# A hybrid decoder block: one column of blocks goes from the seven-product scheme to plain products, and the state space steps get another order and a third buffer

## The chip, the cores and the metric

The kernel runs on one core of one Trainium2 chip, in float32. The metric is the time on the device in microseconds (us). The engines are PE (TensorE, matmuls), DVE (VectorE), ACT (ScalarE), POOL (GpSimd) and SP (SyncE, which here only issues DMAs). Each works through its own queue in the order in which the program is written; they wait for each other by semaphores.

## The reference

One decoder block over 1024 positions of width 1024. The part that matters here is the mixer:

```python
def mixer_block(xn, ...):
    proj = jnp.einsum('bsd,de->bse', xn, w_in) + b_in
    u_ssm, c_bgate, c_cgate, c_val, g_ssm, g_conv = jnp.split(proj, SPLIT_POINTS, axis=-1)
    y_ssm = s5_branch(u_ssm, ...)                       # diagonal state space scan, 32 groups of 64 states
    z = jax.nn.gelu(y_ssm)
    y_a = (z @ w_glu_a) * jax.nn.sigmoid(z @ w_glu_b)
    y_b = (c_bgate * causal_short_conv(c_cgate * c_val, conv_w, conv_b)) @ w_conv_out
    merged = jax.nn.sigmoid(g_ssm) * y_a + jax.nn.sigmoid(g_conv) * y_b
    return merged @ w_out
```

Before it stands an RMS norm, after it a residual, a second norm, a squared-ReLU MLP of width 4096 and a last norm.

## The kernel before

**Exact products from split operands.** Every float32 operand is cut into a high part (an ACT copy with rounding) and a low part (a DVE subtraction). A product of two blocks is three matmuls of 128x512: high by high, high by low, low by high (lines 135 to 137 in `products`, 885 to 887 in `chain`).

**Plain jobs.** `order` lists jobs (`u` 3, then `gs`, `gc`, `bg`). A job multiplies one 128-column block of `w_in` (tile `wr`, cut into `wh` on ACT at line 95 and `wl` on DVE at line 96) with all of x: 48 matmuls into two banks `ps`. Jobs 0 and 1 use the operands `xg` from the start of the kernel. Between them `normed_in` loads x once more, multiplies it by the norm (line 1068) and cuts it into the tiles `xhwB`/`xlwB` (lines 744 and 736) which jobs 2 to 22 use.

**Work beside the products.** The generators `cut_u` and `ssm_step` are drawn piece by piece between matmuls. Each `yield` with a positive number is a declared cost in us, paid out of a credit that grows with the matmuls at the rate `BESIDE` of the job; a negative number is a distance in PE time that must pass first. What is left when the last job begins is written out in one piece by `drain`.

**State space.** `ssm_params` is a chain of some 200 small POOL operations (16 or 32 columns) on columns of one tile, `scratch`, which comes from the same pool of 34 tiles (`unit`, 128x1024) as the operands; so do the small tiles `iota_i` and `bbt`. A tile taken from a pool waits until the last reader of its former owner is done. `cut_u` then copies the first four jobs' results into `U` with 32 copies on ACT and 32 on DVE. Each of eight `ssm_step`s writes its small matrices `Bk` and `Vk` on POOL (`outer`, lines 463 to 467), its angles on DVE and ACT, transposes on PE (`pst`, with `psk` beside it), copies them on ACT (`WT`, `Mk`), projects on PE (`psxr`, `psxi`), rotates and scans on DVE (lines 527 to 540), rotates back (lines 543 to 545 on POOL, 546 to 548 on DVE) and forms its output on PE (`psy`). Step s+1 is started when the projection of step s has been written.

**Groups of seven products.** The other weight blocks go four at a time through a scheme with seven block products (`P1` to `P7`) in place of eight: a group is 84 matmuls. There are two groups (`val`, `cg`) for each of four columns m, a gate group, and four groups for the convolution's output matrix (`rg<-in_wco`). Their operands are sums of blocks; those of the convolution (`xcd`) are made by `conv_first` and `conv_second`, one step after each product, cut into two parts, sent through DRAM by POOL's queue and read back by `xc_load` on SP's queue at the places that `XC_LOADS` names. `group_load` loads a group's raw weights, two groups ahead.

Of the kernel before, what the change touches and what calls it, by code (L numbers as in the profile page):

```python
# [30 lines left out]
PREPARE = 38.0  # L31
N_WARM = 9

BESIDE = {"u": 0.4, "gs": 0.8, "gc": 0.8, "bg": 0.8}
# [12 lines left out]
def block_kernel(ctx, tc, x_t, par, ssm, w_u, win, wco, wglu, wo, w1, w2, out):  # L47
# [97 lines left out]
    order = [("u", 3)] + [("gs", i) for i in range(7)] + [("gc", i) for i in range(7)] + [("bg", i) for i in range(8)]  # L145
    base = {"u": 0, "bg": 4, "cg": 12, "val": 20, "gs": 28, "gc": 36}
# [73 lines left out]
    def cut_u():  # L220
        for b in range(4):
            u = unit(f"U{b}").rearrange("p (q c) -> p q c", q=4)
            tv = ut[b].rearrange("p (c j) -> p j c", j=CH)
            for q in range(4):
                for j in range(CH):
                    o, i = u[32 * j:32 * j + 32, q, :], tv[32 * q:32 * q + 32, j, :]
                    bias = pt[32 * q:32 * q + 32, C_BIN + b:C_BIN + b + 1]
                    if (q + j) % 2:
                        A.activation(o, i, AF.Identity, bias=bias)
                    else:  # L230
                        V.tensor_scalar(o, i, bias, None, op0=ALU.add)
                yield 0.6
            U[b] = u
# [5 lines left out]
    def sp(name, w=NQ):  # L239
        if name not in names:  # L240
            if name in ("th", "tl", "mags"):
                names[name] = spool.tile([P, w], F32, name=f"sp_{name}")
            else:
                o = scratch["used"]
                scratch["used"] = o + w
                names[name] = scratch["t"][:, o:o + w]
        return names[name]
# [10 lines left out]
    Vk2 = [spool.tile([P, 2, 2, 160], F32, name=f"Vk{i}") for i in range(2)]  # L258
    Mk2 = [spool.tile([P, 2, P], F32, name=f"Mk{i}") for i in range(2)]
# [48 lines left out]
    def ssm_params():  # L308
        scratch["t"] = unit("scratch")
        nc.sync.dma_start(bc_raw, ssm.rearrange("p (f q c) -> p f q c", f=4, q=NQ))  # L310
        ii = unit("iota_i").bitcast(I32)[:, :NC]
# [103 lines left out]
        u1 = unit("bbt")[:, :NQ * 16].rearrange("p (q c) -> p q c", q=NQ)  # L415
# [32 lines left out]
    def ssm_step(s):  # L448

        q = slice(2 * s, 2 * s + 2)  # L450
        Vk, Mk = Vk2[s % 2], Mk2[s % 2]
# [21 lines left out]
        yield -3.0  # L473
# [40 lines left out]
        for m in range(4):  # L514
            A.activation(Mk[32 * m:32 * m + 32, :, 32 * m:], pk[:, :, :P - 32 * m], AF.Copy)
        yield -4.0
# [6 lines left out]
        if s < 7:  # L523
            start(ssm_step(s + 1))
# [17 lines left out]
        yr, t2, t3 = sh(f"yr{s}"), sh(f"t2{s}"), sh(f"t3{s}")  # L542
        G.tensor_tensor(t2, xr, sn, op=ALU.mult)  # L543
        G.tensor_tensor(t3, xi, cs, op=ALU.mult)
        G.tensor_tensor(t3, t3, t2, op=ALU.add)
# [4 lines left out]
        yield -6.0  # L550

        py = bank(f"psy{s}")
        for i in range(2):
            o = i * NC
            T.matmul(py[:, o:o + NC], Mk[:, i, :], u_of(2 * s + i), start=True, stop=False)
            for r, y in ((0, yr), (1, t3)):
# [135 lines left out]
    xcd = {(nm, part): scratch_of(f"xc{nm}{part}", (P, 4, HALF)) for nm in X_OF.values() for part in "hl"}  # L692
# [265 lines left out]
    def to_xc(m, name, t, lo=None):  # L958
        split_out(f"xc{name}{m}", lambda part: xcd[name, part][:, m, :], t, lo)
# [31 lines left out]
    def done_cg(m, quad, ps, less):  # L991
# [10 lines left out]
        elif quad == "c21":  # L1002
            conv.append(conv_second(m))
# [37 lines left out]
    for m in range(4):  # L1041
# [49 lines left out]
    for n in range(n_main):  # L1091
# [30 lines left out]
        if n >= n_main - 4:  # L1122
            sums_load(n - (n_main - 4))
        if k == "u":
# [24 lines left out]
    def xc_load(name, u):  # L1149
        ts = []  # L1150
        for part in "hl":
# [4 lines left out]
        xc[name, u] = ts  # L1156

# [20 lines left out]
    for n in range(first_f1):  # L1178
        preps = [group_steps(n, 1), group_steps(n + 1, 0) if n + 1 < first_f1 else iter(())]

        def after(i):
            for prep in preps:
                next(prep, None)
            for _ in range(2 if n == first_co - 1 and i in (1, 2) else 1):
                conv_step()
            step_on()
            for name, u in XC_LOADS.get(7 * (n - first_co + 1) + i, []):
                xc_load(name, u)
            if n >= first_co and i == 1:
                gate_load(n - first_co)  # L1190
            if i == 6 and n + 2 < first_f1:
                group_load(n + 2)
# [522 lines left out]
```

## Time and profile before

| | us |
|---|---|
| median of three runs (lowest, highest) | 1559.28 (1557.91, 1562.05) |
| the profiled execution's own time | 1562.93 |
| its span in the profile | 1560.8 |

The span is the stretch from the first to the last instruction; 2.1 us of the execution lie around it. The profile's page gives busy time by engine, then forty slices of 39 us each; further views give single stretches, waits, and instructions in order of time. The mean of a PE instruction in these views is longer than the distance between two of them, since matmuls are pipelined; the distance between starts is what a matmul costs.

### The profile page before, as it was taken

To read this page: it belongs to the slowest core of one execution; us is meant where nothing else is said; L and a number is where in the kernel's file an instruction comes from. 1 tells how busy PE (TensorE), PEld (TensorE's weight loads), DVE (VectorE), ACT (ScalarE), POOL (GpSimd) and SP (SyncE) were. 2 spreads that over 40 slices of the span, in tenths; PEclk is the share of its full clock that TensorE was granted. 3 is DMA by queue.
4 is the path that set the end of the run, shared out by engine and by line. 5 is a ranking of instruction groups with operands and counts; after the bars stand their busy time and mean duration, and the time that the engine had idled before them with its cause. 6 is when DMAs were issued, how large, how long until landed. Compare 5 with 4: busy or idle time off the path is not lost.

```text
span 1560.8 us, 17513 instructions
## 1 busy us (share of the span) xinstructions
PE 1439.8 (92%) x6407; PEld 1183.6 (76%) x6407; DVE 1026.0 (66%) x1459; ACT 621.7 (40%) x903; POOL 305.1 (20%) x562
## 2 busy tenths in 40 slices
PE   9757999999489997599999999999999999999997
PEld 7645778787368886487888888888888778787887
DVE  7551757777778887155663588777776355858576
ACT  6245345333454444122331245444333342424254
POOL 5860351635102111000000001222222101000000
PEclk9968999999689999799999999999999999999999
DMA  5612212223043556955542124555556658736212
GB/s 205 209 61 90 72 67 96 68 84 146 27 148 140 184 181 251 363 201 197 207 174 104 58 85 137 176 179 186 178 182 233 241 188 200 257 97 254 94 50 100
DMA packets 80518, 240.84 MB, mean 154 GB/s; under 512 B 10160, under 2 KB 18736, under 8 KB 80432
## 3 DMA queue, kind: packets, MB, share of 16 engines
q1 hardware_dynamic: 52016, 158.97, 29.7%
q0 software_dynamic: 18624, 61.88, 11.2%
q10 hardware_dynamic: 9792, 18.88, 3.1%
q8 instruction: 50, 0.82, 0.2%
q14 instruction: 36, 0.29, 0.1%
HBM read 158.94 MB, written 80.74 MB: 154 GB/s over the span
## 4 chain that ended last, share of the span: by engine, by line
PE 71%; DVE 8%; POOL 8%; DMA 5%; ACT 4%; issue 3%; SPq 0%; ACTq 0%; DVEq 0%; POOLq 0%
PE seed L885 6%; PE seed L887 6%; PE seed L886 6%; PE pa L887 4%; PE pa L885 4%; PE pa L886 4%; PE pe L885 4%; PE pe L887 4%; PE pe L886 4%; PE ps L135 2%; PE ps L137 2%; PE ps L136 2%; PE pw L135 2%; PE pw L137 2%; PE pw L136 2%
## 5 line engine op out<-in xcount | busy, mean ns | idle before, releaser
L136 PE MATMUL ps<-xlwB,wh 128*128 128x512 f32 x336 | 136.9, 407 | 20.1 <-DVE xlwB L736 20.1
L135 PE MATMUL ps<-xhwB,wh 128*128 128x512 f32 x336 | 140.3, 418 | 15.8 <-ACT wh L95 11.2
L137 PE MATMUL ps<-xhwB,wl 128*128 128x512 f32 x336 | 135.9, 405 | 0.6 <-DVE wl L96 0.5
L857 DVE TENSOR_TENSOR gl<-gs,gh 128x1024 fp32r<-128x1024 f32 x78 | 95.0, 1218 | 11.0 <-ACT gh L853 11.0
L853 ACT ACTIVATE gh<-gs 128x1024 fp32r<-128x1024 f32 x78 | 82.3, 1055 | 34.4 <-DVE gs L849 27.1
L136 PEld LDWEIGHTS ps<-xlwB,wh 128*128 128x128 f32 x336 | 66.2, 197 | 35.9 <-DVE xlwB L736 22.4
L135 PEld LDWEIGHTS ps<-xhwB,wh 128*128 128x128 f32 x336 | 66.3, 197 | 33.1 <-ACT wh L95 12.0
L96 DVE TENSOR_TENSOR wl<-wr,wh 128x1024 fp32r<-128x1024 f32 x23 | 29.6, 1286 | 78.4 <-ACT wh L95 78.4
L137 PEld LDWEIGHTS ps<-xhwB,wl 128*128 128x128 f32 x336 | 66.3, 197 | 16.0 <-DVE wl L96 1.7
L857 DVE TENSOR_TENSOR gl<-rg,gh 128x1024 fp32r<-128x1024 f32 (+1 forms) x78 | 72.1, 950 | 5.3 <-ACT gh L853 4.6
L896 ACT ACTIVATE seed<-pa 128x512 f32<-128x512 f32 x39 | 22.7, 582 | 117.5 <-PE pa L887 117.1
L853 ACT ACTIVATE gh<-rg 128x1024 fp32r<-128x1024 f32 (+1 forms) x78 | 62.8, 838 | 0.4 <-ACT e L1135 0.4
L1135 ACT ACTIVATE e<-ps,pt 128x512 f32<-128x512 f32 x42 | 28.8, 687 | 59.1 <-PE ps L137 54.2
L543 POOL TENSOR_TENSOR t<-xr,sn 128x512 f32<-128x512 f32 x8 | 12.0, 1506 | 200.6 <-DVE xr L540 200.6
L135 PE MATMUL pw<-mh,hwo 128*128 128x512 f32 x128 | 49.9, 390 | 0.0
L137 PE MATMUL pw<-mh,lwo 128*128 128x512 f32 x128 | 49.8, 389 | 0.0
L136 PE MATMUL pw<-ml,hwo 128*128 128x512 f32 x128 | 49.8, 389 | 0.0
L885 PE MATMUL seed<-xhft,gh 128*128 128x512 f32 x112 | 44.4, 397 | 3.3 <-DVE holdc L1487 3.3
L886 PE MATMUL seed<-xlft,gh 128*128 128x512 f32 x112 | 44.2, 395 | 0.0
L887 PE MATMUL seed<-xhft,gl 128*128 128x512 f32 x112 | 44.1, 394 | 0.0
L887 PE MATMUL pa<-xhfB,gl 128*128 128x512 f32 x112 | 43.6, 389 | 0.0
L886 PE MATMUL pa<-xlfB,gh 128*128 128x512 f32 x112 | 43.6, 389 | 0.0
(648 smaller groups left out, 4311.1 us busy)
## 6 DMA issues: line engine op xcount, KB each, us to landing
rg<-in_w SPq DMA_DIRECT2D x52, 512.0 KB, 4.5
wr<-in_win SPq DMA_DIRECT2D x23, 512.0 KB, 3.5
rg<-in_win SPq DMA_DIRECT2D x18, 512.0 KB, 4.2
xn<-in_x_t SPq DMA_DIRECT2D x16, 256.0 KB, 4.3
xnd<-xn ACTq DMA_DIRECT2D x16, 256.0 KB, 3.1
bgd<-e ACTq DMA_DIRECT2D x16, 256.0 KB, 2.0
xnr<-xnd SPq DMA_DIRECT2D x8, 512.0 KB, 5.2
bgt<-bgd SPq DMA_DIRECT2D x8, 512.0 KB, 3.9
```

The costliest lines, as they stand in the source:

```text
L96: V.tensor_sub(lo, r, hi.bitcast(F32))
L135: T.matmul(ps, wh[:, j, :], xh[:, cols], start=start and i == 0, stop=False)
L136: T.matmul(ps, wh[:, j, :], xl[:, cols], start=False, stop=False)
L137: T.matmul(ps, wl[:, j, :], xh[:, cols], start=False, stop=stop and i == n - 1)
L543: G.tensor_tensor(t2, xr, sn, op=ALU.mult)
L853: A.activation(hi[nm], src[nm], AF.Copy)
L857: V.tensor_sub(lo[nm], src[nm], hi[nm].bitcast(F32))
L885: T.matmul(p, wh[:, kb, :], xh, start=first and kb == 0, stop=False, skip_group_check=True)
L886: T.matmul(p, wh[:, kb, :], xl, start=False, stop=False, skip_group_check=True)
L887: T.matmul(p, wl[:, kb, :], xh, start=False, stop=kb == 3, skip_group_check=True)
L896: A.activation(seed, pa, AF.Copy, scale=-1.0)
L1135: A.activation(t, src, AF.Identity if k == "bg" else AF.Sigmoid, bias=col(C_BIN + base[k] + i))
```

## The change

- Column m = 0 of `val` and `cg` leaves the groups of seven (`for m in range(1, 4)`), and its four blocks become four more plain jobs at the end of `order`: 4 x 48 matmuls for 2 x 84.
- `scratch`, `iota_i` and `bbt` come from the work tiles of the state space steps (`sh`, a ring of twelve 128x512 tiles) and no longer from `unit`.
- `cut_u` declares 2.0 for each piece in place of 0.6; the rates and distances change (`BESIDE`, `PREPARE`, the negative yields).
- `ssm_step(s + 1)` is started before the projection of step s; `Vk` and `Mk` get a third buffer.
- The three rotating products of lines 543 to 545 move from POOL to DVE.
- Three of the seven convolution operands (`B22`, `t3`, `t4`) are stored whole and cut after loading (`xc_cut`), and the weights of the second output group are loaded earlier, at step 4 of the gate group in place of step 6.

```diff
-PREPARE = 38.0
+PREPARE = 32.0
...
-BESIDE = {"u": 0.4, "gs": 0.8, "gc": 0.8, "bg": 0.8}
+BESIDE = {"u": 0.4, "gs": 0.84, "gc": 0.84, "bg": 0.84, "val": 0.8, "cg": 0.5}
...
+    order += [(k, i) for k in ("val", "cg") for i in (0, 4)]
...
-                yield 0.6
+                yield 2.0
...
-                names[name] = scratch["t"][:, o:o + w]
+                if o % HALF + w > HALF:
+                    o = o // HALF * HALF + HALF
+                    scratch["used"] = o + w
+                if o % HALF == 0:
+                    scratch["t"] = sh(f"scratch{o}")
+                names[name] = scratch["t"][:, o % HALF:o % HALF + w]
...
-    Vk2 = [spool.tile([P, 2, 2, 160], F32, name=f"Vk{i}") for i in range(2)]
-    Mk2 = [spool.tile([P, 2, P], F32, name=f"Mk{i}") for i in range(2)]
+    Vk2 = [spool.tile([P, 2, 2, 160], F32, name=f"Vk{i}") for i in range(3)]
+    Mk2 = [spool.tile([P, 2, P], F32, name=f"Mk{i}") for i in range(3)]
...
-        scratch["t"] = unit("scratch")
...
-        ii = unit("iota_i").bitcast(I32)[:, :NC]
+        ii = sh("iota_i").bitcast(I32)[:, :NC]
...
-        u1 = unit("bbt")[:, :NQ * 16].rearrange("p (q c) -> p q c", q=NQ)
+        u1 = sh("bbt")[:, :NQ * 16].rearrange("p (q c) -> p q c", q=NQ)
...
-        yield -3.0
+        yield -6.0
...
+        if s < 7:
+            start(ssm_step(s + 1))
         yield -4.0
...
-        if s < 7:
-            start(ssm_step(s + 1))
...
-        yr, t2, t3 = sh(f"yr{s}"), sh(f"t2{s}"), sh(f"t3{s}")
-        G.tensor_tensor(t2, xr, sn, op=ALU.mult)
-        G.tensor_tensor(t3, xi, cs, op=ALU.mult)
-        G.tensor_tensor(t3, t3, t2, op=ALU.add)
+        yr, t2 = sh(f"yr{s}"), sh(f"t2{s}")
         V.tensor_mul(yr, xr, cs)
         V.tensor_mul(t, xi, sn)
         V.tensor_sub(yr, yr, t)
         yield 1.9
-        yield -6.0
+        V.tensor_mul(t2, xr, sn)
+        V.tensor_mul(t, xi, cs)
+        V.tensor_add(t, t, t2)
+        yield 1.9
+        yield -4.0
...
+    XC_SPLIT = ("B11", "t1", "B21", "n2")
...
     def to_xc(m, name, t, lo=None):
+        if name not in XC_SPLIT:
+            nc.gpsimd.dma_start(xcd[name, "r"][:, m, :], t)
+            return
...
-        elif quad == "c21":
+        elif quad == ("c21" if m else "c22"):
             conv.append(conv_second(m))
...
-    for m in range(4):
+    for m in range(1, 4):
...
+        if k in ("val", "cg"):
+            for hh in range(2):
+                (done_val if k == "val" else done_cg)(0, f"c{1 + i // 4}{1 + hh}", ps[hh], None)
+            continue
...
+    def xc_cut(name):
+        for u in range(2):
+            t, = xc[name, u]
+            hi = unit(f"xhc{name}{u}", F32R)
+            A.activation(hi, t.bitcast(F32), AF.Copy)
+            low.append((t, t.bitcast(F32), hi))
+            lows(1)
+            xc[name, u] = [hi, t]
+        lows()
...
+            if i == (4 if n == first_co - 1 else 6) and n + 2 < first_f1:
+                group_load(n + 2)
...
+            if n == first_co and i in (0, 3, 5):
+                xc_cut({0: "B22", 3: "t3", 5: "t4"}[i])
...
-            if i == 6 and n + 2 < first_f1:
-                group_load(n + 2)
```

**On PE, before the last plain job.** Before the change this stood on PE at the end of the products: the output of step 6, then all of step 7, and only then the first matmul (`ps_0`) of the last job.

```order
L137 MATMUL ps_1_2948<-xhwB_934,wl_2804 128x512
L555 MATMUL psy_3058<-U_1067,Mk_203 128x256
...
L557 MATMUL psy_3058<-t_2926,Vk_201 128x255
L506 MATMUL pst_3072<-ident,Bk 128x128 x4
L509 MATMUL psk_3073<-Vk_202,Bk 32x128 x4
L522 MATMUL psxr_3087<-U_1067,WT 128x256
...
L555 MATMUL psy_3115<-U_1067,Mk_204 128x256
L557 MATMUL psy_3115<-yr_3106,Vk_202 128x255
...
L135 MATMUL ps_0_3048<-xhwB_785,wh_2943 128x512
```

After the change the output of step 7 stands within the second half (`ps_1`) of the third last job; the two jobs behind it follow without a state space matmul.

```order
L137 MATMUL ps_1_3193<-xhwB_821,wl_3099 128x512
L561 MATMUL psy_3249<-U_1193,Mk_205 128x256
L563 MATMUL psy_3249<-yr_3173,Vk_202 128x255
L563 MATMUL psy_3249<-t_3138,Vk_202 128x255
...
L135 MATMUL ps_1_3193<-xhwB_908,wh_3098 128x512
```

No matmul of the steps is left for `drain`: 108 product matmuls stand behind the last `psy`. Before, the transposes of the eight steps stood 96 to 120 product matmuls apart; now 96 to 132 apart.

**On ACT, in job 2.** Before the change these rows stood between the weight copy (`wh`) for job 3 and the one for job 4; `e` is the activation of job 2's result.

```order
L95 ACTIVATE wh_960<-wr_729 128x1024
L229 ACTIVATE U_980<-ut_609,pt 32x256 x8
L229 ACTIVATE U_1009<-ut_612,pt 32x256 x8
L229 ACTIVATE U_1038<-ut_615,pt 32x256 x8
L229 ACTIVATE U_1067<-ut_835,pt 32x256 x4
L1135 ACTIVATE e_0_1076<-ps_0_966,pt 128x512
...
L95 ACTIVATE wh_1082<-wr_842 128x1024
```

After the change:

```order
L95 ACTIVATE wh_962<-wr_731 128x1024
L230 ACTIVATE U_982<-ut_614,pt 32x256 x8
L230 ACTIVATE U_1035<-ut_617,pt 32x256 x2
L1152 ACTIVATE e_0_1040<-ps_0_968,pt 128x512
...
L95 ACTIVATE wh_1046<-wr_844 128x1024
```

Of the 32 copies on ACT, 28 stood ahead of job 4's weights and 4 behind; now they go 10, 8, 10 and 4 over four jobs.

**On SP, the convolution's operands.** Before the change (h and l are the parts, r is a whole operand, `rg` are the second output group's weights):

```order
L1154 DMA xlcn_4577<-xcn2l 128x1024
L1154 DMA xhcB_4605<-xcB22h 128x1024
L1154 DMA xlcB_4607<-xcB22l 128x1024
...
L1154 DMA xhct_4633<-xct3h 128x1024
L1154 DMA xlct_4635<-xct3l 128x1024
...
L810 DMA rg_0_4645<-in_wco 128x256 x4
L810 DMA rg_1_4650<-in_wco 128x256 x4
L1154 DMA xhct_4675<-xct3h 128x1024
```

After the change:

```order
L1171 DMA xlcB_4496<-xcB21l 128x1024
L820 DMA rg_0_4513<-in_wco 128x256 x4
L820 DMA rg_1_4518<-in_wco 128x256 x4
L1171 DMA xhcn_4529<-xcn2h 128x1024
L1171 DMA xlcn_4531<-xcn2l 128x1024
L1171 DMA xrcB_4553<-xcB22r 128x1024
L1171 DMA xhcB_4555<-xcB21h 128x1024
L1171 DMA xlcB_4557<-xcB21l 128x1024
L1171 DMA xrct_4575<-xct3r 128x1024
```

The weights have moved ahead of nine loads of operands (twelve before), and the 28 loads have become 22.

## Rows read from the trace of the kernel before

**Rows 1.** Page, part 1: busy time, share of span, instructions by engine.
```profile
PE 1439.8 (92%) x6407; PEld 1183.6 (76%) x6407; DVE 1026.0 (66%) x1459; ACT 621.7 (40%) x903; POOL 305.1 (20%) x562
```

**Rows 2.** Stretches: length, busy time by engine (x instructions), PE clock, DMA share, GB/s.
```profile
60.00:140.00 80.00, 43.61 (x151) 31.87 (x150) 36.56 (x62) 40.15 (x54) 38.80 (x112) 0.74 0.33 112
140.00:382.00 242.00, 233.40 (x1031) 191.07 (x1030) 162.63 (x233) 95.82 (x143) 97.72 (x132) 0.96 0.25 89
382.00:425.00 43.00, 19.40 (x72) 14.94 (x71) 32.48 (x52) 15.82 (x27) 7.67 (x5) 0.72 0.11 38
...
440.00:605.00 165.00, 164.96 (x717) 135.90 (x716) 135.28 (x171) 77.48 (x107) 25.17 (x46) 0.98 0.46 161
605.00:668.00 63.00, 39.00 (x128) 29.48 (x127) 23.00 (x31) 12.76 (x20) 5.95 (x11) 0.78 0.96 352
```

**Rows 3.** Waits of PE: who waited for whom, us in total, times, longest.
```profile
PE ps L136 <- DVE xlwB L736: 20.1, 4, 15.8
...
PE psk L509 <- POOL Vk L467: 8.6, 5, 2.2
PE seed L885 <- DVE gatec L1016: 7.8, 1, 7.8
PE pa L885 <- ACT gh L853: 6.7, 2, 5.9
```

**Rows 4.** Timeline of PE, 55 to 135: start, length, line, tiles, [idle before].
```profile
55.69 0.39 PE L1103 MATMUL ps<-xh,wh 128*128 128x512 f32 x1
...
64.30 0.39 PE L1105 MATMUL ps<-xh,wl 128*128 128x512 f32 x1
...
98.60 0.80 PE L136 MATMUL ps<-xlwB,wh 128*128 128x512 f32 x1 [0.89 <-DVE xlwB L736]
...
99.62 0.63 PE L135 MATMUL ps<-xhwB,wh 128*128 128x512 f32 x1
...
103.89 0.63 PE L136 MATMUL ps<-xlwB,wh 128*128 128x512 f32 x1
...
129.19 0.79 PE L135 MATMUL ps<-xhwB,wh 128*128 128x512 f32 x1 [10.82 <-ACT wh L95]
...
134.46 0.63 PE L137 MATMUL ps<-xhwB,wl 128*128 128x512 f32 x1
```

**Rows 5.** Timeline of ACT, 90 to 110.
```profile
94.65 0.63 ACT L744 ACTIVATE xhwB<-xn 128x512 fp32r<-128x512 f32 x1 [20.29 <-POOL sp_tl L280]
...
104.70 5.30 ACT L229 ACTIVATE U<-ut,pt 32x256 f32<-32x256 f32 x7
```

**Rows 6.** Timeline of DVE, 70 to 90.
```profile
72.59 0.74 DVE L1068 SCALAR_TENSOR_TENSOR xn<-xn,pt,rstd 128x512 f32<-128x512 f32 x1
87.33 0.88 DVE L736 TENSOR_TENSOR xlwB<-xn,xhwB 128x512 fp32r<-128x512 f32 x1 [13.99 <-POOL bbi L280]
```

**Rows 7.** Timeline of PE, 388 to 422, the last state space step.
```profile
388.40 1.06 PE L509 MATMUL psk<-Vk,Bk 128*32 128x128 f32 x8
403.07 1.22 PE L522 MATMUL psxr<-U,WT 128*128 128x256 f32 x2 [13.61 <-ACT WT L512]
...
421.63 0.68 PE L135 MATMUL ps<-xhwB,wh 128*128 128x512 f32 x1
```

**Rows 8.** Groups of DVE by line and shape, 140 to 440: busy us, mean ns.
```profile
L547 DVE TENSOR_TENSOR t<-xi,sn 128x512 f32<-128x512 f32 x8 | 14.2, 1771 | 0.0
L546 DVE TENSOR_TENSOR yr<-xr,cs 128x512 f32<-128x512 f32 x8 | 13.7, 1715 | 0.0
L548 DVE TENSOR_TENSOR yr<-yr,t 128x512 f32<-128x512 f32 x8 | 13.3, 1662 | 0.3
...
L491 DVE TENSOR_TENSOR a<-a,k 128x512 f32<-128x512 f32 x8 | 6.1, 761 | 0.3
...
L533 DVE TENSOR_TENSOR xi<-xi,t 128x512 f32<-128x512 f32 x8 | 5.5, 692 | 0.3
```

**Rows 9.** Waits of DVE, 560 to 720.
```profile
DVE gs L845 <- DMA rg<-in_wco: 21.1, 1, 21.1
```

More of the change, by code (lines that the diff above doesn't have):

```diff
@@ L450, in ssm_step @@
         q = slice(2 * s, 2 * s + 2)
-        Vk, Mk = Vk2[s % 2], Mk2[s % 2]
+        Vk, Mk = Vk2[s % 3], Mk2[s % 3]
         if s == 0:
@@ L555, in ssm_step @@
             T.matmul(py[:, o:o + NC], Mk[:, i, :], u_of(2 * s + i), start=True, stop=False)
-            for r, y in ((0, yr), (1, t3)):
+            for r, y in ((0, yr), (1, t)):
                 T.matmul(
@@ L691, in block_kernel @@
     gd = {(k, i): scratch_of(f"{k}d{i}") for k in ("gs", "gc", "bg") for i in range(8)}
-    xcd = {(nm, part): scratch_of(f"xc{nm}{part}", (P, 4, HALF)) for nm in X_OF.values() for part in "hl"}
+    XC_SPLIT = ("B11", "t1", "B21", "n2")
+    xcd = {
+        (nm, part): scratch_of(f"xc{nm}{part}", (P, 4, HALF))
+        for nm in X_OF.values() for part in ("hl" if nm in XC_SPLIT else "r")
+    }
     zd = [scratch_of(f"zd{i}") for i in range(4)]
@@ L1150, in xc_load @@
         ts = []
-        for part in "hl":
+        for part in "hl" if name in XC_SPLIT else "r":
             t = unit(f"x{part}c{name}{u}", F32R)
```

## The prediction

> **What bounds the kernel.** I read the page first: PE is busy for 1439.8 us of the span and the other engines for much less [rows 1]. So the time is PE's work plus PE's stops, and the question is in which stretch it stops. The table of stretches answers [rows 2]: 440 to 605 is full at a clock of 0.98, but 60 to 140 has 43.6 busy us of 80 at a clock of 0.74, 382 to 425 has 19.4 of 43, and 605 to 668 has 39 of 63, with the DMA engines at 0.96. Between, 140 to 382 looks full, yet lost some: 0.96 of the clock. All of the change lies before 668, so I read PE's waits and its rows in order of time there [rows 3, 4, 7].
>
> A 128x512 matmul costs what lies between two starts: 38 steps from 55.69 to 64.30, or 0.227 us. After a stop they start 0.427 us apart: ten steps from 99.62 to 103.89 [rows 4]. These are the upper and the lower of the two levels of the clock (2.4 and 1.2 GHz); each time PE had stood still before. So a stop costs its length and then 0.2 us for each slow matmul.
>
> **Parameters' scratch, 73 to 104.** Job 2 needs the low parts of x; its longest wait is 15.8 us of the 20.1 for `xlwB` [rows 3]. DVE stood for 13.99 us until POOL was done with `bbt`, and ACT for 20.29 us until POOL's last operation on `scratch` [rows 5, 6]: no data passes there, only tiles. POOL's chain itself still ends near 94; its first reader is state space step 0, whose angles DVE would reach some 20 us later, about 175 product matmuls into the jobs. With the wait gone, what is late next is the loading and cutting of x. At 72.59 ten operations were still to do, four products of 0.74 and six subtractions of about 0.7 [rows 6], so the last low part comes near 79.6 if its loads hold out, instead of 98.6 [rows 4]: 19.0 us. At least eleven slow matmuls behind it become fast, 2.2 us. Gain 21; bounds 13 (the loads are late, the clock falls anyway) and 24.
>
> **Thinner `cut_u`, 118 to 135.** PE waits 10.82 us for the weight copy of job 4 [rows 4], since 28 copies of 0.75 us stand before it on ACT (seven took 5.30, [rows 5]). In the new order ten do, 7.6 us, less than the 10.9 us (48 x 0.227) that a job lasts. Twelve slow matmuls follow the stop (to 134.46, [rows 4]), 2.4 us. Gain 13; bounds 9 (a low part still a little late in each of four jobs) and 13.
>
> **The last step off the path, 389 to 422.** From the end of `psk` at 389.5 to the last job's start at 421.63 [rows 7] PE does only step 7's projection and output, about 4.5 us of matmuls at the upper level (they took 3.6 us for the projection alone at the lower). The rest, 27.7, and some 1.3 us of slow matmuls behind, go, because `psy` of step 7 now has 108 product matmuls behind it and its latency is covered by them. Gain 29; bounds 20 and 29, by whether the earlier steps slip.
>
> **Steps that overlap, DVE in place of POOL, 140 to 382.** PE waited five times for `Vk`, 8.6 us [rows 3]: POOL could write it only after the scan and the three rotating products. Now POOL starts the next step's matrices right after `psk`. With the slow matmuls after those stops I take 13; bounds 5 and 17. On DVE, 24 products are added. But the 24 that ran beside POOL's took 1.66 to 1.77 us each, and the same shape without POOL takes 0.69 [rows 8]. So 41.2 us become 16.6, and the new ones add 16.6: DVE's sum falls by 8 us and stays near 160 of 242 us.
>
> **Column 0 as plain jobs.** 192 matmuls for 168, all at 0.227: 24 more, a loss of 5.4. Their weights are as many bytes. They also give the steps 43 us more of cover, which is what the term of the last step uses.
>
> **The convolution's operands, 605 to 668.** The DMA engines are full here, 352 GB/s [rows 2]. Six loads of 512 KB and, in the last column, three stores of 256 KB go: 3.9 MB, 11 us. DVE waited 21.1 us for the second group's weights [rows 9], which stood last; now they go ahead, and 1.05 MB delay the operands behind them by 3 us. The stop of 7.8 us for `gate` [rows 3] was for a tile whose former owner, a part of `B22`, was still being stored through the same queues; that store no longer exists. Against this stand six copies on ACT and six subtractions on DVE, which lie beside two or three products each. I take 10; bounds 0 and 20.
>
> **Into the first group.** PE waited 5.9 us for `gh` at 439 [rows 3], behind step 7's leftovers on ACT. These are gone: I take 4, bounds 0 and 7.
>
> **Allowance.** Eight steps now run closer together, and `psy` of a step with a gelu beside it stands 96 matmuls (22 us) after its projection, against some 21 us of DVE work (162.6 of 242 us [rows 2], a step each 31 us). I charge 5 us; bounds 0 and 12.
>
> **Sum.** 21 + 13 + 29 + 13 - 5.4 + 10 + 4 - 5 = 79.6. From the profiled execution's own 1562.9 this gives 1483.3. The median of the runs lies 3.6 below the profiled execution; I give 1481.
>
> **Rivals.**
> *DVE becomes the bound (1510).* POOL's matrices now always run beside DVE's rotations. POOL was busy 97.7 us from 140 to 382 [rows 2]; less the 24 moved products, some 40 us, seven steps' matrices take 8 us each. If DVE stood still for all of that, its 21 us between projection and `psy` would be 29 against 22 us of cover and what the next step may slip, and PE would stop for 4 us or more eight times, near 30 us with the slow matmuls. Against it: the subtraction that runs beside the matrices takes 0.761 us and not 0.692 [rows 8], a tenth longer, not twice.
> The Trainium skill (SBUF — State Buffer, "Who interferes with whom") speaks for this rival: of a GpSimd operation and a VectorE operation with two SBUF inputs, the later is blocked until the first ends. By it the three products cost DVE what the rows show, but the matrices would too, and the time would be 1510; the row just named shows a tenth, so I keep the sum.
> *The convolution gains nothing (1495).* The whole operands must be cut before use. ACT's copy of `B22` stands ahead of the copy that frees the bank of P5; if its load is late, ACT stands and PE with it. The term falls from 10 to -4.
> *More than I count (1466).* The convolution's stretch and the seam both reach their upper bounds, 13 us, and half of the allowance is not used.
> *Slower than before (1563 or more).* The ring of twelve work tiles is the place: a step takes fourteen. POOL's outer products for step s+1 take over tiles that DVE's last products of earlier steps read. If DVE is a whole step late, POOL starts only after it, then PE's transposes, ACT's copy, the projection and DVE again follow in a row, and overlap is lost. The price is about POOL's 8 us and 2 us of slow matmuls a step; from 10 us a step on, eight steps eat the 80 us. Against it: in the order the former owner is read a step earlier, 30 us before.
> That the tiles' wait stays (another former owner) is excluded by the order: the new owners of these tiles follow operands of jobs 0 and 1, which PE leaves by 64.3 [rows 4].
>
> **Chances.** Forecast (1470 to 1495) 0.53; DVE bound 0.13; convolution 0.16; more 0.12; slower 0.04; between slower and these 0.02. The range 1462 to 1510 holds the forecast, the two middle rivals up to their times and most of the upper gain, a little over 0.8. A measurement of this kernel can tell about 0.3% from no change: faster 0.94, same 0.02, slower 0.04.
>
> **What would show it.** Right: no wait of ACT or DVE for POOL between 60 and 100, and PE at `xlwB` until about 80; no stop over 2 us near the fourth job's weights; no `psk` wait for POOL; the last `psy` followed by product matmuls without a stop; DVE's six rotating products near 0.7 us; fewer than 20 lost us around the convolution's group, with the DMA engines still full. Wrong: `psy` waiting for DVE in most steps; a `gh` wait at the seam longer than before; ACT waiting for a load of `B22`; or new stops where the four plain jobs meet the sums of x.

## The result and the profile after

| | before | after |
|---|---|---|
| median of runs, us | 1560.62 (4 runs, 1557.91 to 1562.05) | 1491.23 (4 runs, 1487.85 to 1492.04) |
| profiled execution: own time, span, us | 1562.93, 1560.8 | 1492.04, 1490.3 |

After stands to before as 0.9553, with a 95% interval from 0.9532 to 0.9574: 69.4 us less between the medians, where the sum of the forecast was 79.6.

Stretches of after, cut where the work of [rows 2] now lies, with the same columns:

```profile
60.00:140.00 80.00, 68.45 (x275) 53.09 (x274) 47.29 (x75) 49.90 (x68) 39.96 (x100) 0.87 0.39 134
140.00:380.00 240.00, 240.00 (x1098) 198.87 (x1097) 167.97 (x285) 105.99 (x158) 57.95 (x104) 1.00 0.27 95
380.00:425.00 45.00, 39.48 (x171) 31.33 (x169) 39.54 (x62) 24.66 (x38) 0.33 (x1) 1.00 0.38 129
...
540.00:600.00 60.00, 39.79 (x145) 28.89 (x144) 29.41 (x36) 17.36 (x22) 4.85 (x9) 0.83 0.87 310
```

The steps' stretch is full at the upper clock, and the drain of the last step is gone. What is left stands at both ends: PE is idle for 11.6 us in 60 to 140 and for 20.2 us around the convolution's group (540 to 600). A new place is 400 to 440, where PE is idle for 7.7 us (the rows are in experiment 8). PE's waits name the three places (columns as in [rows 3]): `xlwB` in the first, `gl` and one wait for `sv` in the new one, B21 and another `sv` in the last.

```profile
PE pa L895 <- DMA xhcB<-xcB21h: 12.6, 2, 9.9
PE ps L136 <- DVE xlwB L746: 10.5, 5, 3.7
PE seed L895 <- ACT sv L923: 6.4, 2, 4.1
PE pa L897 <- DVE gl L867: 5.8, 4, 2.4
```

The waits for `Vk` and for the fourth job's weights are gone, and the one for `gate` is down to 0.6 us.

**Lost time.** To weigh each term I choose product matmuls of 128x512 that do the same work in both kernels, as marks. The time from one mark to the next, less 0.2267 us for each product started in between (the distance of two starts at the upper clock), is what was lost there: stops, slow matmuls, and also the state space matmuls, which are not products. These rows of PE's timeline are the marks, of before:

```profile
65.05 0.50 PE L135 MATMUL ps<-xhwB,wh 128*128 128x512 f32 x1 [0.35 <-ACT wh L95]
...
110.04 0.39 PE L135 MATMUL ps<-xhwB,wh 128*128 128x512 f32 x1
...
137.74 0.39 PE L135 MATMUL ps<-xhwB,wh 128*128 128x512 f32 x1
...
384.65 0.40 PE L137 MATMUL ps<-xhwB,wl 128*128 128x512 f32 x1
...
432.62 0.39 PE L137 MATMUL ps<-xhwB,wl 128*128 128x512 f32 x1
...
459.01 0.39 PE L885 MATMUL pa<-xhwB,gh 128*128 128x512 f32 x1
...
725.68 0.39 PE L135 MATMUL pgb<-zh,hglu 128*128 128x512 f32 x1
```

and of after, where 384.65 has no counterpart:

```profile
65.40 0.50 PE L135 MATMUL ps<-xhwB,wh 128*128 128x512 f32 x1 [0.54 <-ACT wh L95]
...
97.49 0.39 PE L135 MATMUL ps<-xhwB,wh 128*128 128x512 f32 x1
...
111.09 0.39 PE L135 MATMUL ps<-xhwB,wh 128*128 128x512 f32 x1
...
404.14 0.39 PE L137 MATMUL ps<-xhwB,wl 128*128 128x512 f32 x1
...
431.30 0.40 PE L895 MATMUL pa<-xhwB,gh 128*128 128x512 f32 x1
...
653.06 0.39 PE L135 MATMUL pgb<-zh,hglu 128*128 128x512 f32 x1
```

The first mark is job 2's first product. The next two are 60 and 120 products later; a job has 48, so they lie in jobs 3 and 4. 384.65 is the last product ahead of the drain (the 959th behind the first). 432.62 and 404.14 are the last products of the plain jobs (1007 and 1199 behind the first). Then come the second group's first product and the first product of `z @ w_glu_b` (`pgb`), called the gates here. Two examples: job 2 of before, 110.04 - 65.05 - 60 x 0.2267 = 31.4, of after 97.49 - 65.40 - 13.6 = 18.5. Eight steps of after, from 111.09 to 404.14 with 1079 products: 293.05 - 244.6 = 48.5, or 6.06 a step, which is their own matmuls without a stop (2.41 of them the step's output, `psy`).

| term | forecast | measured | from |
|---|---|---|---|
| scratch, job 2 | 21 | 12.9 | 31.4 to 18.5 |
| thinner `cut_u`, job 4 | 13 | 14.1 | 14.1 to 0 |
| steps 0 to 6 | 13 | 16.7 | 246.91 - 839 x 0.2267 = 56.7, where seven steps at 6.06 less the last output's 2.4 need 40.0 |
| last step | 29 | 28.6 | 47.97 - 48 x 0.2267 = 37.1, where a step and that output need 8.5 |
| 24 more matmuls | -5.4 | -5.4 | counted |
| first group (seam) | 4 | -0.8 | 432.62 to 459.01 and 404.14 to 431.30, less 17.0 for 75 matmuls (the last plain product, two into `seed`, the group's own 72): 9.4 to 10.2 |
| convolution's groups | 10 | 6.8 | from there to the gates, 266.67 less 1020 products and 221.76 less 852: 35.4 to 28.6 |
| allowance | -5 | 0 | no wait for `psy` |

The measured terms give 72.9; job 2 starts 0.35 later, so the gates begin 72.6 us earlier (725.68 against 653.06). Two us are given back behind them, in work that the change doesn't touch; why is not shown.

### The profile page after: what moved, and what is told of

The parts are those of the page before. It is cut to its first block, busy times and chain, and to the rows that moved or that the text cites. A ratio compares the mean times of both kernels' runs of the same rounds, so it can differ in the third digit from the quotient of the medians.

```text
span 1490.3 us, 17454 instructions
## 1 busy us (share of the span) xinstructions
PE 1428.7 (96%) x6431; PEld 1176.5 (79%) x6431; DVE 1001.7 (67%) x1461; ACT 617.7 (41%) x890; POOL 265.0 (18%) x528
## 4 chain that ended last, share of the span: by engine, by line
PE 85%; DVE 6%; DMA 5%; issue 2%; ACT 1%; SPq 0%; DVEq 0%; ACTq 0%
PE ps L135 6%; PE seed L895 6%; PE ps L136 6%; PE ps L137 6%; PE seed L896 6%; PE seed L897 6%; PE pa L897 4%; PE pa L896 4%; PE pa L895 4%; PE pe L896 4%; PE pe L895 4%; PE pe L897 4%; PE pw L135 2%; PE pw L136 2%; PE pw L137 2%
## 5 line engine op out<-in xcount | busy, mean ns | idle before, releaser
L136 PE MATMUL ps<-xlwB,wh 128*128 128x512 f32 x400 | 158.7, 397 | 10.5 <-DVE xlwB L746 10.5
L135 PE MATMUL ps<-xhwB,wh 128*128 128x512 f32 x400 | 161.2, 403 | 0.5 <-ACT wh L95 0.5
L137 PE MATMUL ps<-xhwB,wl 128*128 128x512 f32 x400 | 158.2, 396 | 0.5 <-DVE wl L96 0.5
L136 PEld LDWEIGHTS ps<-xlwB,wh 128*128 128x128 f32 x400 | 76.2, 191 | 29.2 <-DVE xlwB L746 13.8
L867 DVE TENSOR_TENSOR gl<-gs,gh 128x1024 fp32r<-128x1024 f32 x74 | 90.2, 1219 | 9.1 <-ACT gh L863 9.1
L863 ACT ACTIVATE gh<-gs 128x1024 fp32r<-128x1024 f32 x74 | 78.0, 1054 | 35.6 <-DVE gs L859 27.3
L135 PEld LDWEIGHTS ps<-xhwB,wh 128*128 128x128 f32 x400 | 76.4, 191 | 18.3 <-issue 1.2
L137 PEld LDWEIGHTS ps<-xhwB,wl 128*128 128x128 f32 x400 | 76.4, 191 | 17.0 <-DVE wl L96 1.0
L96 DVE TENSOR_TENSOR wl<-wr,wh 128x1024 fp32r<-128x1024 f32 x27 | 33.9, 1255 | 62.8 <-ACT wh L95 62.7
L895 PE MATMUL pa<-xhfB,gh 128*128 128x512 f32 x112 | 43.6, 389 | 0.0
```

Of the source, the lines that this page charges most:

```text
L96: V.tensor_sub(lo, r, hi.bitcast(F32))
L135: T.matmul(ps, wh[:, j, :], xh[:, cols], start=start and i == 0, stop=False)
L136: T.matmul(ps, wh[:, j, :], xl[:, cols], start=False, stop=False)
L137: T.matmul(ps, wl[:, j, :], xh[:, cols], start=False, stop=stop and i == n - 1)
L863: A.activation(hi[nm], src[nm], AF.Copy)
L867: V.tensor_sub(lo[nm], src[nm], hi[nm].bitcast(F32))
```

## Experiments

All are the changed kernel with one edit unless said. They are read by their ratio to before and by the same lost times. How far a single profile can be trusted shows where kernels have the same code. Eight of them lost 16.0 to 18.5 us over the first 60 products from job 2 on, so less than 3 us at that place tells nothing; after itself is the highest of the eight. Seven lost 38.4 to 40.1 us from the first group to the gates (after 38.8), and nine lost 48.4 in the steps.

**1. The scratch alone undone.**

```diff
...
-                names[name] = scratch["t"][:, o % HALF:o % HALF + w]
+                names[name] = scratch["t"][:, o:o + w]
...
+        scratch["t"] = unit("scratch")
...
-        ii = sh("iota_i").bitcast(I32)[:, :NC]
+        ii = unit("iota_i").bitcast(I32)[:, :NC]
...
-        u1 = sh("bbt")[:, :NQ * 16].rearrange("p (q c) -> p q c", q=NQ)
+        u1 = unit("bbt")[:, :NQ * 16].rearrange("p (q c) -> p q c", q=NQ)
```

> The changed kernel with the parameters' scratch, the integer ramp and the product tile back in the large pool (that part of the change alone undone). Theory from the two traces: the part is worth the 12.9 us by which PE's lost time at job 2 fell, so 1503 to 1506, with VectorE waiting for POOL again near 73. Rival one, the size forecast: 21 us, 1510 to 1514. Rival two: with the second and third tile of the steps' work in use elsewhere, other owners take these tiles and the wait falls on something that nobody needs soon: under 4 us, 1490 to 1495.

Measured: 1505.4 us, ratio 0.9644 [0.9615, 0.9672]; 30.2 lost at job 2. VectorE's longest waits from 60 to 105 show the old one back (waiting line, releaser, us in total, times, longest):

```profile
DVE xlwB L742 <- POOL bbi L281: 13.2, 1, 13.2
```

So the wait comes from the place of these three tiles alone. The part is worth some 13 us, not 21: 11.7 to 14.2 by the lost times (30.2 against 16.0 to 18.5), 14.2 by the medians.

**2. Why not 21.** In after, VectorE stops on its way through x for loads; its timeline, and the rows of SP's that issue them:

```profile
66.63 0.33 SPq L87 DMA_DIRECT2D wr<-in_win  x1
67.01 9.79 SPq L1080 DMA_DIRECT2D xn<-in_x_t  x8
```

```profile
71.06 0.75 DVE L1081 SCALAR_TENSOR_TENSOR xn<-xn,pt,rstd 128x512 f32<-128x512 f32 x1 [4.46 <-DMA xn<-in_x_t]
...
78.61 0.81 DVE L1081 SCALAR_TENSOR_TENSOR xn<-xn,pt,rstd 128x512 f32<-128x512 f32 x1 [1.01 <-DMA xn<-in_x_t]
79.35 1.10 DVE L746 TENSOR_TENSOR xlwB<-xn,xhwB 128x512 fp32r<-128x512 f32 x1
...
83.56 3.03 DVE L746 TENSOR_TENSOR xlwB<-xn,xhwB 128x512 fp32r<-128x512 f32 x3
```

SP issues in order: a weight load at 66.63, which had waited for its tile, and only then the second half's x. The last low part ends at 86.6, not 79.6, and behind the first of its five stops PE starts products 0.427 us apart, the lower clock, until 91.98. The edit puts four of the loads first (`xn_load` issues one, and `normed_in` then takes its tile):

```diff
+        if n == 1:
+            for j in range(4):
+                xn_load(4 + j // 2, j % 2)
         w_load(n + 2)
```

> The changed kernel with one edit: in job 1 the first four loads of x for the second half go to SP's queue ahead of the two weight loads. Theory: the term for the parameters' scratch came out at 12.9 us and not 21 because VectorE, once free of POOL, stands 4.5 us at 66.6 for a load of x that SP issues only at 67.0, behind a weight load that waits for its tile until the copies of the weights before are done; then the loads come some 6 us sooner, that wait and the 1.0 us at 78.6 go, and with 2 to 3 us of matmuls at the lower clock the time falls by 5 to 9 us, to 1482 to 1486. Rival one: the loads are late for their own tiles or the DMA engines' sake, and nothing is won: 1490 to 1492. Rival two: the weights of job 3 come late instead, a new stop there, 1491 to 1496.

Measured: 1486.9, ratio 0.9529 [0.9502, 0.9555], 0.9 above the theory's range and with an interval that overlaps after's; the trace decides: 11.2 lost at job 2 against 16.0 to 18.5, and the gates begin 8.3 us earlier. SP issues twelve loads in one run, and the weights, 0.33 us at 65.5, come in time:

```profile
47.00 16.21 SPq L1081 DMA_DIRECT2D xn<-in_x_t  x12
65.52 0.33 SPq L87 DMA_DIRECT2D wr<-in_win  x1
```

The queue's order was 5 to 7 us of the missing 8 (11.2 against 16.0 to 18.5).

**3. `cut_u` alone undone.**

```diff
-                yield 2.0
+                yield 0.6
```

> The changed kernel with the cutting of U offered at its old cost, so that 28 copies stand on ScalarE ahead of a weight copy again. Theory: the 14.1 us at job 4 return: 1502 to 1507, with one stop of 10 to 11 us there and slow matmuls behind it. Rival: since low parts of x and the jobs come earlier now, the copies have U's products earlier too and end in time: 1489 to 1494.

Measured: 1508.6, ratio 0.9669 [0.9651, 0.9687], 1.6 above the theory's range. From the 60th to the 120th product 14.8 are lost, where after loses none, with one wait of PE:

```profile
PE ps L135 <- ACT wh L95: 11.9, 1, 11.9
```

So the term doesn't depend on the other parts.

**4. The overlap alone undone** (late start, two buffers).

```diff
-        if s < 7:
-            start(ssm_step(s + 1))
         yield -4.0
...
+        if s < 7:
+            start(ssm_step(s + 1))
         xr, xi, t = sh(f"xr{s}"), sh(f"xi{s}"), sh(f"t{s}")
```

> The changed kernel with each state space step started only after the projection of the one before, and two buffers in place of three (the overlap alone undone; the plain jobs and VectorE's rotating products stay). Theory: the overlap gave the stops between the steps back (16.7 us with what lay behind them), while the last step's drain is covered by the plain jobs: 1500 to 1510, stops at the matrices of 1 to 2 us again, and the last output still followed by products. Rival one: the drain too came from the overlap, so 45 us return: 1530 to 1540. Rival two: with the rotations off POOL its matrices come in time anyway: 1490 to 1495.

Measured: 1491.8, ratio 0.9553 [0.9529, 0.9577], after's own; the steps lose 48.4 as in after. The theory falls, and the second rival holds: with the other parts in place, the early start and the third buffer can go and nothing is lost.

**5. The rotating products back on POOL**, overlap kept.

```diff
-        V.tensor_mul(t2, xr, sn)
-        V.tensor_mul(t, xi, cs)
-        V.tensor_add(t, t, t2)
+        G.tensor_tensor(t2, xr, sn, op=ALU.mult)
+        G.tensor_tensor(t3, xi, cs, op=ALU.mult)
+        G.tensor_tensor(t3, t3, t2, op=ALU.add)
```

> The changed kernel with the three rotating products of each step back on POOL (early start and three buffers stay). After the run that undid the overlap and lost nothing, two theories are left for the 16.7 us that the steps gave back. One: the products off POOL gave it; with them back, POOL's matrices of the next step stand ahead of the products, the two engines slow each other, and the output waits for the products: stops at the output matrices and 8 to 17 us more, 1498 to 1508. Two: either part is enough, since with the early start POOL makes its matrices before the scan ends: 1489 to 1494, VectorE's products beside POOL's again at 1.7 us.

Measured: 1493.9, ratio 0.957 [0.9546, 0.9595]; the steps lose 51.0, 2.6 more. The second theory seemed right: either part is enough.

**6. Both undone**: the edits of experiments 4 and 5 together.

> The changed kernel with both parts of the steps' new order undone: the three rotating products on POOL, each step started after the projection, two buffers. Each part undone alone gave back under 3 us between the steps (lost time from job 2 to the last job, less what was lost at job 2: 48.4, 48.4 and 51.1 us). Theory: either part is enough, since POOL is late only where the products stand ahead of its matrices; with both undone the stops at the matrices return and the steps lose 60 to 66 us: 1500 to 1508. Rival: the 16.7 us came from neither but from the jobs' pace and the freed tiles: 1489 to 1494.

Measured: 1496.2, ratio 0.9591 [0.9574, 0.9609], between the theory's range and the rival's; the steps lose 52.4, 3.9 more and not 12 to 18. The theory falls too: neither part is needed. Yet VectorE's products beside POOL's take as long as in [rows 8] (groups by line and shape, 140 to 400):

```profile
L552 DVE TENSOR_TENSOR t<-xi,sn 128x512 f32<-128x512 f32 x8 | 14.2, 1777 | 0.0
```

so VectorE's slow products were not what cost PE the 16.7 us. POOL's timeline tells more. In before, around step 1's stop, the products stand ahead of the next matrices:

```profile
179.44 1.50 POOL L543 TENSOR_TENSOR t<-xr,sn 128x512 f32<-128x512 f32 x1 [74.99 <-DVE xr L540]
...
184.28 0.85 POOL L463 TENSOR_TENSOR o<-dsc_r,bbr 128x128 f32<-128x128 f32 x1
...
194.38 1.09 POOL L467 TENSOR_TENSOR Vk<-o 64x160 f32<-64x160 f32 x2
```

PE asks for `Vk` at 193.7 and goes on at 195.52; POOL had stood 75 us for the scan, with these matrices queued behind its products. With both undone, the matrices of step 1 stand first:

```profile
135.75 1.34 POOL L472 TENSOR_TENSOR Bk<-o 64x128 f32<-64x128 f32 x2 [34.47 <-PE psk L514]
...
142.15 1.10 POOL L472 TENSOR_TENSOR Vk<-o 64x160 f32<-64x160 f32 x2
150.15 1.50 POOL L548 TENSOR_TENSOR t<-xr,sn 128x512 f32<-128x512 f32 x1 [6.90 <-DVE xr L545]
```

PE needs them only near 162. What is left of the change in the steps are the numbers that pace them: `BESIDE` 0.84 for 0.8, and a distance of 6 us for 3 between the matrices and the angles. (The scratch and `cut_u`, each undone alone in experiments 1 and 3, leave the steps at 48.4.) What these numbers do can be read off the order of POOL's instructions, without a run. In before the matrices stand behind the products of the step before in steps 1, 2, 4 and 6, the four in which PE stopped (at 195.52, 227.04, 292.85 and 358.81); in the kernel of this experiment in none. With 0.8 put back in it they do in all seven, with 3 us put back too in just those four, with 3 us alone in none. So the pace sets the order, and where the order is before's, PE stopped. That the old pace would bring the stops back to this kernel was not run: that the pace prevents them here is argued by exclusion and by the order, and not shown.

The pace is not the only part that would do, though. With the old pace put back in the kernel of experiment 5, which keeps the early start, the matrices still stand ahead of the products in all seven steps; and with the products on VectorE nothing stands ahead of them on POOL. By the order, then, the early start and the new pace are each enough, and the moved products may be. Undoing some of them, as experiments 4 to 6 do, shows that these are not needed, and not that they do nothing.

**7. Column 0 back in groups.**

```diff
-    order += [(k, i) for k in ("val", "cg") for i in (0, 4)]
-    for m in range(1, 4):
+    for m in range(4):
-        elif quad == ("c21" if m else "c22"):
+        elif quad == "c21":
```

> The changed kernel with column 0 back in groups of seven products (23 plain jobs, convolution of column 0 as before). Theory: the last step's 28.3 us were given back by the cover of the four plain jobs; step 7 starts some 1030 product matmuls in, the last job would begin after 960, so all of step 7 is drained again in front of it: stops of 10 to 14 us at the projection and the output, 28 to 36 us back, less 5.4 for 24 matmuls and 3 to 5 at the seam: 1510 to 1520. Rival: the earlier and closer steps end in time by themselves, and the plain jobs only cost: 1483 to 1488.

Measured: 1512.9, ratio 0.9692 [0.9668, 0.9715]; the steps lose 78.9, 30.4 more. Of PE's timeline from 330 to 392 these are the stops over 2 us:

```profile
350.93 1.22 PE L562 MATMUL psy<-yr,Vk 128*128 128x255 f32 x2 [8.75 <-DVE yr L549]
354.47 1.22 PE L562 MATMUL psy<-t,Vk 128*128 128x255 f32 x2 [2.32 <-DVE t L553]
360.87 0.73 PE L528 MATMUL psxr<-U,WT 128*128 128x256 f32 x2 [2.69 <-ACT WT L516]
371.85 1.22 PE L562 MATMUL psy<-yr,Vk 128*128 128x255 f32 x2 [6.87 <-DVE yr L549]
```

PE stops for the latency of steps 6 and 7 again. So it is the cover of the four plain jobs that gives the last step's 28.6 us, as forecast.

**8. The seam.** In after VectorE is busy for 18.45 and 19.27 of the 20 us from 400 and from 420, and PE stops:

```profile
400.00:420.00 20.00, 16.47 (x71) 12.60 (x70) 18.45 (x27) 10.32 (x15) 0.00 (x0) 1.00 0.53 177
420.00:440.00 20.00, 15.88 (x65) 12.70 (x64) 19.27 (x24) 8.51 (x13) 3.92 (x7) 0.91 0.50 167
```

```diff
-            for _ in range(2 if n == first_co - 1 and i in (1, 2) else 1):
+            for _ in range(0 if n == 0 else 2 if n == first_co - 1 and i in (1, 2) else 1):
                 conv_step()
```

> The changed kernel with one edit: no step of the gated convolution in the first group (column 0's begins one group later). Theory: the seam lost 10.2 us in the first group since VectorE is busy for 37.7 of the 40 us from 400 to 440 and the plain jobs made column 0's convolution fall there; without its some 7.5 us of work in that group the stops of 2.4, 1.0 and 4.1 us and the slow matmuls behind them go: 5 to 10 us less, 1481 to 1486. Rival: the work only moves into the next groups and stops PE there, or column 3 is stored later and the convolution's group waits longer: 1489 to 1497.

Measured: 1488.3, ratio 0.9528 [0.9505, 0.955], not told from after by time. From the first group to the gates 35.7 are lost against 38.8, 2.7 below the lowest kernel with after's code. `sv` no longer stops PE for 4.1 there; a stop of 2.05 at 460.8, for `sv` again, takes part of it back. Theory and rival each have a part.

**9. All seven operands in two parts.**

```diff
-    XC_SPLIT = ("B11", "t1", "B21", "n2")
+    XC_SPLIT = tuple(X_OF.values())
...
-            if n == first_co and i in (0, 3, 5):
+            if False:
                 xc_cut({0: "B22", 3: "t3", 5: "t4"}[i])
```

> The changed kernel with all seven convolution operands stored and loaded as two parts (no cutting behind the load; the second output group's weights stay ahead). Theory: 3.9 MB more pass through DMA engines that are full there, so the 7.2 us that the stretch gave back go: 1496 to 1501. Rival one, the size forecast for the bytes alone: 11 us, 1501 to 1504. Rival two: what the bytes give, the cut behind the load takes (ScalarE waited 17 us for a load of B22): 1488 to 1493.

Measured: 1495.5, ratio 0.9584 [0.9559, 0.9608]; first group to gates 43.7, 4.9 more than after and 3.6 more than the highest kernel with after's code. The stop for `gate` is back (7.8 in [rows 3]):

```profile
PE seed L895 <- DVE gatec L1029: 6.5, 1, 6.5
```

Storing three operands whole is worth some 4 to 5 of the 6.8; a size between the theory's and the second rival's.

**10. The second output group's weights later.**

```diff
-            if i == (4 if n == first_co - 1 else 6) and n + 2 < first_f1:
+            if i == 6 and n + 2 < first_f1:
```

> The changed kernel with the second output group's weights issued two products later, behind the operands again. Theory from the trace: in their early place these eight loads hold SP for 16 us, 7.8 of them for a tile that VectorE frees, with the second part of B21 behind them, for which PE then waits 9.9 us; issued later, that wait falls to 3 us or less while VectorE's wait for the weights comes back: 3 to 7 us less, 1484 to 1488. Rival, the forecast's reading: weights last cost VectorE some 20 us there and PE 3 us or more: 1494 to 1498. Third: the DMA engines are full either way and the order decides nothing: 1489 to 1493.

Measured: 1488.9, ratio 0.9541 [0.9515, 0.9568]; first group to gates 38.3 against 38.8. PE's wait for B21 falls from 12.6 to 5.7, and a wait of 3.4 for `xcn2h` and others come. That is the third theory: the order decides nothing that these runs can tell.

**11. Edits 2, 8 and 10 together**, with the four early loads those of the first halves, and in job 1 all first halves ahead of the second.

> The changed kernel with three edits: four loads of x, those of the first half's lower blocks, ahead of the weights, and in job 1 all first halves before the second ones; no step of the convolution in the first group; the second output group's weights two products later. Alone, the first gave about 6 us at job 2 and the second 3.1 from the first group to the gates, the third 0.5. Theory: they lie in different stretches and add, and the order of the halves gives 2 to 4 more: 1476 to 1481. Rival: the lost time only moves to the convolution's group, which waits for DMA in any case: 1484 to 1488.

Measured: 1482.3, ratio 0.9498 [0.9476, 0.9521], the fastest here, its interval below after's, and a little above the theory's range. At job 2 13.0 are lost, not told from the 11.2 of edit 2 alone: the stops for `xlwB` are shorter, and one at the next weights is new. From the first group to the gates 34.5 are lost.

```profile
PE ps L135 <- ACT wh L95: 4.4, 1, 4.4
```

**12. The same, and the sums of x one job earlier.**

```diff
-            if n >= n_main - 3:
-                sums_of(n - (n_main - 3))
+            if n >= n_main - 4:
+                sums_of(n - (n_main - 4))
```

> The kernel with the three edits and a fourth: the sums of x are loaded and made one job earlier each, so that no sums are left for the first group. Theory: VectorE is the limit of the first group, and 4.8 us of its work go from there to jobs in which it is busy 70 to 85 per cent; the remaining stop of 2.4 us with its slow matmuls goes: 2 to 5 us below the kernel with three edits, 1472 to 1478. Rival: those jobs have no room for it, or the loads of the sums collide with tiles still in use, and new stops come ahead of the groups: 1478 to 1485.

Measured: 1493.2, ratio 0.9569 [0.955, 0.9589], 11 us more than without. SP's longest wait from 340 to 412, and PE's from 60 to 740:

```profile
SPq L1097 <- PE ps L137: 37.3, 1, 37.3
```

```profile
PE pa L895 <- ACT gh L863: 9.6, 1, 9.6
```

A load of the sums waits for a tile that PE reads to the end of the plain jobs, and the first group's weights stand behind it on SP. That is the rival's second reason, at more than the price it gave (1478 to 1485).

## Why the forecast came out as it did

**Scratch.** Right in mechanism, mis-sized: 12.9 for 21 (some 13 by experiment 1 too). The step that failed is "the last low part comes near 79.6 if its loads hold out". They didn't: SP had them behind a weight load (experiment 2). The bound of 13 was the case that came. The other slip in it, that eleven slow matmuls become fast, fell too: PE stopped five times and ran slowly to 91.98.

**`cut_u`.** Right, 14.1 for 13 (a little above its upper bound), and independent of the rest (experiment 3).

**The last step.** Right, 28.6 for 29, by the cover that was named (experiment 7).

**Steps that overlap.** The wait and its price were read rightly, 16.7 for 13, and the state that was described came: POOL's matrices are made long before PE asks. The step that failed is what was to bring this about. "POOL starts the next step's matrices right after `psk`" was put down to the early start, the third buffer and the moved products; experiments 4 to 6 take these away singly and together and lose 0, 2.6 and 3.9 us of the 16.7. The two numbers of the pace, which the prediction passed over, are enough in their place, by the order of POOL's instructions. How the 16.7 us divide among parts of which more than one is enough can't be said. That the size came out although one of these parts was not seen is luck. The products on VectorE became as cheap as forecast, 0.68 to 0.75 us each, but with the new pace in place that is worth only 2.6 to 4 us (experiment 5 against after, 6 against 4).

**Convolution.** Mis-sized, 6.8 for 10. Some 4 to 5 come from the operands stored whole, the stop for `gate` with them (experiment 9). The order of the weights, for which 3 were charged, made no difference that could be told (experiment 10). Against the gain, PE's waits for B21 grew from 5.7 us in before to some 15, which the sum didn't have; its stop of 7.9 us for `gl` (before, at 662.8) went. The sign "fewer than 20 lost us, with the DMA engines still full" was just missed: 20.2 us idle at a DMA share of 0.87. The second rival's sign, ScalarE standing for B22, did come:

```profile
568.97 1.06 ACT L1179 ACTIVATE xhcB<-xrcB 128x1024 fp32r<-128x1024 f32 x1 [17.04 <-DMA xrcB<-xcB22r]
```

but PE itself waited for B21 until 572.63 (9.9 us). For the bank, freed behind the second such wait, it stopped for 1.2 us (at 582.35).

**Seam.** Wrong: -0.8 for 4. The leftovers of step 7 went, and what is late next was not asked: column 0's convolution, which the plain jobs start, falls into the group in which VectorE makes the last sums of x and the group's weights. That it does is shown only in part: without these steps of the convolution some 3 us come back (experiment 8). The prediction's last sentence on what would show it wrong named this place, and the sum did not charge it.

**Allowance.** Not used. PE never waits for `psy` in after.

**Sum.** The measured terms give 72.9 of the 79.6. Scratch, convolution and seam came out 16.1 us short, the unused allowance, the steps and `cut_u` gave 9.8 back: that the sum is near is in part luck. Two us more were lost behind the gates. The median lay 0.8 below the profiled execution, not 3.6 as before the change, and 1483.3 less 3.6 is 1479.7, not 1481.

**Rivals.** VectorE did not become the bound. Beside POOL's matrices stands the last sum of the rotation; the difference ahead of it has no POOL beside it:

```profile
L554 DVE TENSOR_TENSOR t<-t,t 128x512 f32<-128x512 f32 x8 | 6.0, 753 | 0.3
L550 DVE TENSOR_TENSOR yr<-yr,t 128x512 f32<-128x512 f32 x8 | 5.5, 692 | 0.3
```

Six of the eight sums run beside matrices and take 0.77 us, the two others 0.69. The prediction's 0.761 was a mix of this kind and read too low. Of those eight, the four beside matrices took 0.83 and the others 0.69, so the price was a fifth and not a tenth; two of before's rows:

```profile
161.26 0.69 DVE L491 TENSOR_TENSOR a<-a,k 128x512 f32<-128x512 f32 x1
...
191.03 0.83 DVE L491 TENSOR_TENSOR a<-a,k 128x512 f32<-128x512 f32 x1
```

That is still far from the 8 us a step that the rival needs. The Trainium skill (SBUF — State Buffer, "Who interferes with whom") says that a VectorE operation with two SBUF inputs contends with a GpSimd one that reads SBUF; the trace agrees in that VectorE's are slower beside POOL's, 0.77 to 0.83 us against 0.69 here.

The ring of twelve tiles did hold POOL up in after. The matrices' first product waits in six steps for a tile that VectorE's rotation of an earlier step reads (POOL's waits, 90 to 420):

```profile
POOL o L468 <- DVE t L552: 76.0, 6, 18.1
```

POOL works far enough ahead that PE never waited for it, so the price of the last rival was not paid.

## What to carry to other kernels

When a wait is taken away, ask what is late next on every queue, not only on the engine that waited: here a load stood behind another load on SP, and a group found its helper engine full. Where a schedule is paced by numbers, put them back before the credit goes to the visible edit; and where several parts of a change are each enough, undoing one says only that it is not needed. To take work apart into marks of equal work, and to count what lies between, tells terms of some 3 us that medians of four runs don't, once kernels with the same code have shown the spread at that place.

## What was not expected of the hardware

In after POOL's six 128x256 products and sums run beside VectorE's cutting of x, which they had not done before. Alone, from 83.34 to 87.3 of before, they took 0.62 to 0.72 us; beside it they take 1.05 to 1.07, and VectorE's own 128x512 operations 1.10 to 1.21 instead of 0.70 to 0.74. POOL's timeline at the start of it:

```profile
78.84 1.06 POOL L283 TENSOR_TENSOR bbr<-bc_raw,scratch 128x256 f32<-128x256 f32 x1
79.87 1.06 POOL L283 TENSOR_TENSOR bbt<-bc_raw,scratch 128x256 f32<-128x256 f32 x1
```

VectorE's rows from 79.35 (experiment 2) overlap with these in time, and both engines now start an operation every 1.03 us (78.84 to 79.87, 79.35 to 80.37). Alone, the next start came 0.58 us later on POOL (83.34 to 83.92 of before) and 0.6 to 0.7 later on VectorE. So one operation of each takes a little less than the two would one after the other, some 1.2 us. Neither engine shows idle time meanwhile; whether an operation waits within its time for the other engine's or both run slower, these rows can't tell. Work that is merely freed can pay again where it meets the other engine.
